# Hybrid decoder layer, first token tile: sums of squares by products with ones instead of a second load of the rows

## Chip, cores and metric

The kernel runs on one core of a Trainium2 chip. The metric is the device time of one execution in microseconds (us). Beside the plain runs there is one profiled execution with a trace of every engine and every transfer.

## What is computed

One layer on 2048 tokens of width 1024, all in float32. Every row of `x` is first divided by its root mean square; that scale is what the change is about:

```python
def rms_norm(x, w):
    xf = x.astype(jnp.float32)
    y = xf * lax.rsqrt(jnp.mean(xf * xf, axis=-1, keepdims=True) + EPS)
    return (y * w.astype(jnp.float32)).astype(x.dtype)

u = rms_norm(h, norm_pre_mix[i])
proj = u @ w_in[i]
q, k, v, qi, ki, wi, z, xbc, dt = jnp.split(proj, offsets, axis=-1)
```

The projection feeds a sparse attention (an indexer scores all keys, each query keeps its best 256) and a scanned state-space mixer with a short convolution. Their outputs go through one output projection, and a squared-ReLU MLP follows.

## The kernel before

The tokens are cut into four tiles of 512 (T), the 1024 channels into eight tiles of 128 (k). `in_proj(t)` makes, for one token tile, one small product called the misc product here (76 columns: index keys, index weights, step sizes) and 20 products of 128 columns with the tiles of `w_in`. In the back half each token tile gets `out_proj` and `mlp`. Attention, key selection and the scan are generators that `weave` steps beside that main sequence. The order of the instructions on each engine is not written by hand: a scheduler orders them by priorities and its own idea of their durations, and each engine then runs its list in that order, waiting where an operand is not there.

A float32 product is made of three products of rounded halves (`mm3`): high by high (L257), high by low in the moving operand (L260), low by high (L261). For each the moving operand is a channel tile of `x` with 512 tokens, the stationary one a tile of the weights. `moving(t)` (L295 to L313) makes the moving halves: it loads channel tile k of the transposed `x` (name `xr`, ring `wr` of four buffers that the weights share), ACT scales and rounds it to the high half, and DVE (k = 0, 1, 2, 4, 6) or, after one more pass on ACT, POOL (k = 3, 5, 7) makes the low half. `load_w` (L234) loads a half of a weight tile into the same ring and lets ACT (the misc weights) or POOL (L231, L232) make its halves in rings of two (`wh`, `wl`): the third half can only be made once the products that read the first are done.

The scale of the rows is not multiplied into `x`, but into the results. `row_scale(t)` (L276) loads the same 512 rows a second time, not transposed, as four tiles of 128 x 1024 (name `x_in`, ring `m4` of two), squares each on ACT with a sum along the row (L283), and `rsqrt` (L202) turns the four columns of sums into scales with ten small DVE instructions (L210 to L225). `row_spread` (L287) turns them with four products with the identity (`p_rs`, L290) into a tile with the scale along the columns, which DVE copies to `rsb` (L292). Every result is evicted with a multiplication by `rsb` (`scaled`, L329): first that of the misc product (`mi`), then that of each `w_in` product (`raw`). `mi` is transposed by PE (L343) and starts a long list on DVE (L345 to L360 and `softplus`, L437). The two PSUM banks named `mm` go round: misc product, `w_in` tile 0, tile 1, tile 2. Tile 1 needs the bank that `mi` has read; tile 2 needs the bank of tile 0, in which the convolution runs (L372, L374, last written to `pre`).

For token tile 0 all of this stands at the very start of the program; for the later tiles `row_scale(t + 1)` and `moving(t + 1)` are called in the tail of `in_proj(t)` (L429 to L434). `leave` (L525), a step of the scan, already sums squares by products with ones (L532): four products, each with a 128 x 128 tile of squares as the stationary operand and one column of ones as the moving one. All transfers are issued by SP (SyncE), in the order of its list; `late_constants` (L135) loads small constants, `dsk` in two transfers, `dtb` and `nega` among them, and ACT takes the exponential of `nega` (L153).

Of the kernel before, what the change touches and what calls it, by code (L numbers as in the profile page):

```python
# [8 lines left out]
F32 = mybir.dt.float32  # L9
# [6 lines left out]
AF = mybir.ActivationFunctionType  # L16
# [5 lines left out]
P = 128  # L22
L = 2048
D = 1024
T = 512
NT = L // T
NB = T // P
KT = D // P
# [13 lines left out]
def hybrid_layer(ctx, tc, x, x_t, w_cols, n_post_mix, n_post_mlp, w_in, w_misc, dt_bias, a_log, d_skip,  # L42
                 w_out, w_up, w_down, rel_bias, c_ident, c_flip, c_stack, c_tri, c_trineg, c_caus, c_bucket, out, dbg=None):
    nc = tc.nc
    V, S, G, PE, SP = nc.vector, nc.scalar, nc.gpsimd, nc.tensor, nc.sync

    cp = ctx.enter_context(tc.tile_pool(name="cp", bufs=1))
# [27 lines left out]
    def place(tag):  # L75

        if tag in rings:
            rings[tag].append(rings[tag].pop(0))
            return rings[tag][-1]
        return where[tag]  # L80

    def tl(tag, shape, dt=F32, name=None):
        pool, bufs, slot = place(tag)
        return pool.tile(shape, dt, tag=name if tag in ("s", "ks", "ssm") else slot, name=name or tag, bufs=bufs)
# [9 lines left out]
    def once_tile(name, shape, dt=F32):  # L94
        return where["ssm"][0].tile(shape, dt, name=name, bufs=1)
# [6 lines left out]
    def pt(tag, name=None):  # L102
        pool, bufs, slot = place(tag)
        return pool.tile([P, 512], F32, tag=slot, name=name or tag, bufs=bufs)
# [6 lines left out]
    def const(ap, shape, name, dt=F32):  # L111
        t = cp.tile(shape, dt, name=name)
        SP.dma_start(t, ap)
        return t
# [14 lines left out]
    junk_m = cp.tile([P, 512], I8, name="junk_m")  # L129
    tiny = cp.tile([P, 1], F32, name="tiny")  # L130
    V.memset(tiny, 1.17549435e-38)
    w_pm, w_pl, w_ssd = cols[:, 0:8], cols[:, 8:16], cols[:, 56:60]
    cn = {}

    def late_constants():  # L135

        cn["tri"] = once_tile("tri", [P, P])
        SP.dma_start(cn["tri"], c_tri)
        cn["trineg"] = once_tile("trineg", [P, P])
        SP.dma_start(cn["trineg"], c_trineg)  # L140
        cn["ones"] = once_tile("ones", [P, 1])
        V.memset(cn["ones"], 1.0)
        cn["stack"] = const(c_stack, [P, DH], "stack")
        cn["caus"] = const(c_caus, [P, P], "caus")
        dsk = cn["dsk"] = once_tile("dsk", [P, 4])
        for j in range(2):
            SP.dma_start(dsk[j * DH:(j + 1) * DH],
                         d_skip.rearrange("(m j) -> j m", j=2)[j:j + 1].partition_broadcast(DH))
        cn["dtb"] = once_tile("dtb", [P, H])
        SP.dma_start(cn["dtb"], dt_bias.rearrange("(o h) -> o h", o=1).partition_broadcast(P))  # L150
        nega = cn["nega"] = once_tile("nega", [P, H])
        SP.dma_start(nega, a_log.rearrange("(o h) -> o h", o=1).partition_broadcast(P))
        S.activation(nega, nega, AF.Exp)  # L153
        V.tensor_scalar(nega, nega, -1.0, None, op0=OP.mult)
# [47 lines left out]
    def rsqrt(o, v, n, scale, who="s", work=None, also=None):  # L202


        if work is None:
            xx, u = (tl(who, [P, n], name=name) for name in ("rs_x", "rs_u"))
        else:
            xx, u = work[:, 0:n], work[:, n:2 * n]
        yi = tl(who, [P, n], I32, name="rs_y")
        V.tensor_scalar(xx, v, scale, EPS, op0=OP.mult, op1=OP.add)  # L210
        if also is not None:
            V.scalar_tensor_tensor(xx, also, scale, xx, op0=OP.mult, op1=OP.add)
        V.tensor_scalar(yi, xx.bitcast(I32), -0.5, float(0x5f3759df), op0=OP.mult, op1=OP.add)
        y = yi.bitcast(F32)
        q = tl(who, [P, n], name="rs_q")

        V.tensor_tensor(u, xx, y, op=OP.mult)
        V.tensor_tensor(u, u, y, op=OP.mult)
        V.tensor_scalar(q, u, 0.375, -1.25, op0=OP.mult, op1=OP.add)
        V.tensor_tensor(u, u, q, op=OP.mult)  # L220
        V.scalar_tensor_tensor(y, u, 1.875, y, op0=OP.add, op1=OP.mult)

        V.tensor_tensor(u, xx, y, op=OP.mult)
        V.scalar_tensor_tensor(u, u, -0.5, y, op0=OP.mult, op1=OP.mult)
        V.scalar_tensor_tensor(o, u, 1.5, y, op0=OP.add, op1=OP.mult)  # L225
# [25 lines left out]
    state = {"win": "0"}  # L251
# [24 lines left out]
    def row_scale(t):  # L276

        ss = tl("s", [P, NB], name="ss")
        for b in range(NB):
            xt = tl("m4", [P, D], name="x_in")  # L280
            r0 = t * T + b * P
            SP.dma_start(xt, x[r0:r0 + P, :])
            S.activation(xt, xt, AF.Square, accum_out=ss[:, b:b + 1])  # L283
        rs = state["rs", t] = tl("s", [P, NB], name="rs")
        rsqrt(rs, ss, NB, 1.0 / D)

    def row_spread(rs, tag="mm"):  # L287
        p = pt(tag, "p_rs")
        for b in range(NB):
            PE.matmul(p[:, b * P:(b + 1) * P], rs[:, b:b + 1].broadcast_to([P, P]), ident, start=True, stop=True)  # L290
        rsb = tl("rsb", [P, T])
        V.tensor_copy(rsb, p)  # L292
        return rsb

    def moving(t):  # L295

        us = state["u", t] = []
        for k in range(KT):
            d = tl("u", [P, 2, T], F32R)
            raw = tl("wr", [P, T], name="xr")  # L300
            SP.dma_start(raw, x_t[t, :, k, :])
            wk = w_pm[:, k:k + 1]
            if str(k) in MG:
                if MG[0] == "a":
                    S.activation(raw, raw, AF.Copy, scale=wk)
                else:
                    G.tensor_scalar(raw, raw, wk, None, op0=OP.mult)
                S.activation(d[:, 0, :], raw, AF.Copy)
                G.tensor_tensor(d[:, 1, :], raw, d[:, 0, :].bitcast(F32), op=OP.subtract)  # L309
            else:  # L310
                S.activation(d[:, 0, :], raw, AF.Copy, scale=wk)  # L311
                V.scalar_tensor_tensor(d[:, 1, :], raw, wk, d[:, 0, :].bitcast(F32), op0=OP.mult, op1=OP.subtract)  # L312
            us.append(d)  # L313
# [6 lines left out]
    def in_proj(t):  # L320
        t0 = t * T
        w = None
        if t == 0:
            w = load_w(w_misc, [P, KT, 76], '11')
            moving(0)
        else:
            rsb = row_spread(state["rs", t], TB)
        u = state["u", t]
# [2 lines left out]

        p = proj(w_misc, u, w, how=HI_)
        if t == 0:
            row_scale(0)
            rsb = row_spread(state["rs", 0], "acc")
        mi = tl("m2", [76, T], name="mi")
        scaled(mi, p[0:76])
        if t == 0:
            late_constants()
        yield 5.2  # L340
        p = pt(TB, "p_tr")
# [12 lines left out]
        sq = tl("m2", [P, NB, DH], name="sq")  # L354
# [9 lines left out]
        for m in range(8):  # L364
            p = proj(w_in[m], u, how=HI_)
            raw = tl("m2", [P, T + 4], name="raw")
# [8 lines left out]
            if m == 1:  # L375
                p = pt(TB, "p_tr")
# [21 lines left out]
        for m in range(4):  # L398
            p = proj(w_in[8 + m], u, how=HI_)
# [9 lines left out]
        p = proj(w_in[12], u, how=HI_)  # L409
# [8 lines left out]
        p = proj(w_in[13], u, how=HI_)  # L418
# [3 lines left out]
        p = pt(TB, "p_tr")  # L422
# [8 lines left out]
        for m in range(2, 6):  # L431
            queries(m)
            if m == 5 and t + 1 < NT:
                moving(t + 1)  # L434
            yield 5.2
# [22 lines left out]
    def ssd(t):  # L458
# [4 lines left out]
        p = pt(bank, "p_cs")  # L463
# [5 lines left out]
        p = pt(bank, "p_cs")  # L469
# [55 lines left out]
        def leave(c, sis):  # L525

            p = pt(bank, "p_ms")
            for g, si in enumerate(sis):
                ys, sq = si[:, 0:2], si[:, 2:4]
                S.activation(sq, ys, AF.Square)  # L530
                for j in range(2):
                    PE.matmul(p[:, g:g + 1], sq[:, j], cn["ones"], start=j == 0, stop=j == 1)  # L532
            rs = tl("ssm", [P, 2], name="rs_s")
            rsqrt(rs, p[:, 0:2], 2, 1.0 / 256, "ssm", p[:, 2:6])
            for g, si in enumerate(sis):
                ys, yp = si[:, 0:2], si[:, 2:6].rearrange("p (s j) t -> p s j t", s=2).bitcast(F32R)
                sl = slice((g + 1) * P, (g + 2) * P)
                PE.matmul(p[:, sl], rs[:, g:g + 1].broadcast_to([P, P]), ident, start=True, stop=True)
                for j in range(2):
                    V.scalar_tensor_tensor(ys[:, j], ys[:, j], w_ssd[:, 2 * g + j:2 * g + j + 1], p[:, sl],  # L540
                                           op0=OP.mult, op1=OP.mult)
                S.activation(yp[:, 0], ys, AF.Copy)
                V.tensor_tensor(yp[:, 1], ys, yp[:, 0].bitcast(F32), op=OP.subtract)
                r0, t0 = 512 + 256 * g, t * T + c * P
                for s in range(2):
                    SP.dma_start(mix_d[s, r0:r0 + 256, t0:t0 + P].rearrange("(j p) t -> p j t", p=P), yp[:, s].bitcast(F32))
# [541 lines left out]
```

## Time and profile before

| | us |
|---|---|
| median of three runs | 2925.88 |
| lowest and highest of them | 2923.69, 2927.11 |
| the profiled execution, its own time | 2928.29 |
| its span, first to last instruction | 2926.5 |

In the profile, PE is the matrix engine, PEld its weight loads, DVE the vector engine, ACT the scalar engine, POOL GpSimd, SP the engine that issues the transfers. All times are counted from the start of the span. In the timeline a row gives start, duration, engine, line, operation, output and inputs, how many instructions were merged, and in square brackets how long the engine sat idle before and what ended that. One float32 product with a whole float32 operand (lines 290, 343, 532) shows as two records. Products overlap: their rate is read from the distance of their starts, not from their durations.

### The profile page before, as it was taken

What the parts mean: (1) busy time and instruction counts of PE and PEld (TensorE: products, weight loads), DVE (VectorE), ACT (ScalarE), POOL (GpSimd) and SP (SyncE); (2) the same over time, 40 slices, a digit from 0 to 9 for tenths busy, and PEclk for the clock granted to TensorE, in tenths of its full rate; (3) what the DMA queues carried; (4) which work ended last, traced back from release to release, by engine and by line L of the source; (5) the groups of instructions that cost most, each with busy time, mean ns of one, the idle gap of its engine ahead of it and who ended that gap; (6) DMA issues with size and microseconds to landing.
All of it is one profiled execution on the core that took longest, in us unless ns stands there. A gap on an engine that the chain in (4) does not pass through costs nothing.

```text
span 2926.5 us, 41201 instructions
## 1 busy us (share of the span) xinstructions
PE 2761.9 (94%) x13558; PEld 2250.7 (77%) x13558; DVE 1642.4 (56%) x4106; ACT 1481.5 (51%) x2550; POOL 1762.6 (60%) x1721
## 2 busy tenths in 40 slices
PE   7988989789989999998999999999999999999998
PEld 5766767667768887887787888878888888778886
DVE  5479588888575666747765565666444342511113
ACT  2375477675837575677773847644332332311101
POOL 4666556667666656654456575644564656588775
PEclk8999989999989999999999999999999999999999
DMA  3765654634733333255223222553222225522222
GB/s 128 224 189 151 218 157 149 208 118 160 249 120 119 112 103 102 90 176 180 101 94 98 90 97 79 170 177 102 87 95 81 93 78 177 204 95 97 95 94 86
DMA packets 286741, 383.46 MB, mean 131 GB/s; under 512 B 26520, under 2 KB 151360, under 8 KB 286528
## 3 DMA queue, kind: packets, MB, share of 16 engines
q1 hardware_dynamic: 286528, 380.84, 40.0%
q8 instruction: 107, 1.75, 0.2%
q14 instruction: 106, 0.87, 0.1%
HBM read 316.44 MB, written 64.30 MB: 130 GB/s over the span
## 4 chain that ended last, share of the span: by engine, by line
PE 67%; DVE 13%; ACT 6%; DMA 5%; issue 4%; POOL 3%; SPq 1%; POOLq 0%; DVEq 0%; ACTq 0%
PE p_mm L257 9%; PE p_mm L261 9%; PE p_mm L260 9%; PE p_dn L260 7%; PE p_dn L261 7%; PE p_dn L257 7%; ACT junk_k L610 5%; PE p_o L725 4%; PE p_s L683 4%; PE p_pt L717 3%; POOL wl L232 2%; PE p_ix L591 1%; DVE cnd L618 1%; PE p_acc L260 1%; PE p_acc L257 1%
## 5 line engine op out<-in xcount | busy, mean ns | idle before, releaser
L232 POOL TENSOR_TENSOR wl<-wr,wh 128x512 fp32r<-128x512 f32 (+1 forms) x740 | 987.0, 1335 | 179.6 <-ACT wh L229 107.0
L231 POOL TENSOR_SCALAR wh<-wr 128x512 fp32r<-128x512 f32 x674 | 449.6, 667 | 752.1 <-PE p_mm L260 372.8
L257 PE MATMUL p_mm<-u,wh 128*128 128x512 f32 (+1 forms) x1696 | 685.4, 404 | 47.4 <-ACT u L311 15.4
L261 PE MATMUL p_mm<-u,wl 128*128 128x512 f32 (+1 forms) x1696 | 682.8, 404 | 13.2 <-POOL wl L232 12.9
L260 PE MATMUL p_mm<-u,wh 128*128 128x512 f32 (+1 forms) x1696 | 674.9, 398 | 0.6 <-POOL u L309 0.3
L610 ACT ACTIVATE junk_k<-sc,cnd 128x512 int8<-128x512 f32 (+10 forms) x434 | 576.4, 1328 | 157.8 <-DVE cnd L618 122.2
L257 PEld LDWEIGHTS p_mm<-u,wh 128*128 128x128 f32 (+1 forms) x1696 | 322.9, 190 | 119.3 <-ACT u L311 17.5
L260 PE MATMUL p_dn<-wl,g 128*128 128x512 f32 x1008 | 402.2, 399 | 4.2 <-POOL wl L232 4.2
L261 PE MATMUL p_dn<-wh,g 128*128 128x512 f32 x1008 | 399.5, 397 | 2.7 <-POOL g L836 2.7
L261 PEld LDWEIGHTS p_mm<-u,wl 128*128 128x128 f32 (+1 forms) x1696 | 322.5, 190 | 88.7 <-POOL wl L232 21.3
L260 PEld LDWEIGHTS p_mm<-u,wh 128*128 128x128 f32 (+1 forms) x1696 | 322.6, 190 | 69.6 <-DVE u L312 2.3
L257 PE MATMUL p_dn<-wh,g 128*128 128x512 f32 x1008 | 328.0, 398 | 1.9 <-POOL wh L231 1.3
L834 ACT ACTIVATE r<-r 128x512 f32<-128x512 f32 x128 | 80.4, 629 | 437.1 <-DVE r L833 436.7
L688 DVE CUSTOM_DVE_ANT_0 pp<-p_s,mk 128x512 f32<-128x512 f32 (+3 forms) x320 | 192.5, 607 | 134.3 <-PE p_s L683 130.5
L719 ACT ACTIVATE ppt<-p_pt 128x512 fp32r<-128x512 f32 (+1 forms) x288 | 155.3, 568 | 208.1 <-PE p_pt L717 170.0
L720 DVE TENSOR_TENSOR ppt<-p_pt,ppt 128x512 fp32r<-128x512 f32 (+1 forms) x288 | 182.6, 655 | 129.6 <-ACT ppt L719 126.9
L260 PEld LDWEIGHTS p_dn<-wl,g 128*128 128x128 f32 x1008 | 190.3, 189 | 46.8 <-POOL wl L232 5.5
L261 PEld LDWEIGHTS p_dn<-wh,g 128*128 128x128 f32 x1008 | 190.3, 189 | 43.8 <-POOL g L836 3.1
L257 PEld LDWEIGHTS p_dn<-wh,g 128*128 128x128 f32 x1008 | 185.8, 189 | 42.0 <-POOL wh L231 2.9
L725 PE MATMUL p_o<-ppt,VV 128*128 128x256 f32 x1088 | 211.1, 294 | 1.9 <-DVE ppt L720 1.0
L617 DVE TENSOR_SCALAR keep<-cnt 128x1 int32<-128x1 f32 (+1 forms) x341 | 70.2, 206 | 244.1 <-ACT junk_k L610 242.7
L836 POOL TENSOR_TENSOR g<-r,g 128x512 fp32r<-128x512 f32 x128 | 170.1, 1331 | 53.2 <-ACT g L835 51.9
(253 smaller groups left out, 4177.6 us busy)
## 6 DMA issues: line engine op xcount, KB each, us to landing
wr<-w_up SPq DMA_DIRECT2D x256, 256.0 KB, 2.6
wr<-w_down SPq DMA_DIRECT2D x256, 256.0 KB, 2.6
wr<-w_in SPq DMA_DIRECT2D x160, 256.0 KB, 2.9
tq<-toep_d SPq DMA_DIRECT2D x128, 128.0 KB, 2.6
qs<-q_d SPq DMA_DIRECT2D x256, 64.0 KB, 2.5
wr<-w_out SPq DMA_DIRECT2D x64, 256.0 KB, 3.7
mix<-mix_d SPq DMA_DIRECT2D x32, 512.0 KB, 8.1
q_d<-qp SPq DMA_DIRECT2D x24, 512.0 KB, 3.6
```

The source lines that it names most:

```text
L231: G.tensor_scalar(dst_hi, src_f, 1.0, 0.0, op0=OP.mult, op1=OP.add)
L232: G.tensor_tensor(dst_lo, src_f, dst_hi.bitcast(F32), op=OP.subtract)
L257: m = PE.matmul(o, ah, bh, start=first, stop=False)
L260: PE.matmul(o, ah, bl, start=False, stop=False)
L261: state["mm3"] = PE.matmul(o, al, bh, start=False, stop=last).ins.name
L610: S.activation(junk_k[:, 0:n], scs[j], AF.Sign, bias=bias(j), accum_out=cnt[:, j:j + 1])
L683: PE.matmul(p[:, 0:w], qs[:, var, hh, :], K1[:, g, j0:j0 + w], start=var == 0, stop=var == 1)
L688: V.tensor_tensor_reduce(out=pp[:, j0:j0 + w], in0=p[:, 0:w], in1=mk[:, j0:j0 + w], scale=1.0, scalar=-3e38, op0=OP.add, op1=OP.max, accum ...
L719: S.activation(pg[:, 0, 0:w], p[:, 0:w], AF.Copy)
L720: V.tensor_tensor(pg[:, 1, 0:w], p[:, 0:w], pg[:, 0, 0:w].bitcast(F32), op=OP.subtract)
L725: PE.matmul(po[:, c0:c0 + 256], VV[:, kk, g, :], pg[:, part, j * 256:(j + 1) * 256], start=kk == 0 and part == 0, stop=kk == nb - 1 and pa ...
L836: G.tensor_tensor(gt[:, 1, :], r, gt[:, 0, :].bitcast(F32), op=OP.subtract)
```

## The change

For token tile 0, `moving(0, sums)` squares each channel tile right after its load (ACT, a new 128 x 512 tile `sq0` of the ring `m4`), and PE multiplies it with a column of ones: for each k four products, one for each block of 128 tokens, with the squares as the stationary operand. The eight k are summed in PSUM (`p_ss`, a bank of the pair `acc`). `rsqrt` reads those four columns and keeps its two work tiles in the same bank. `row_scale(0)` and its four loads of `x_in` are gone. The column of ones is made once at the start, in another pool, and `leave` uses it too. Token tiles 1 to 3 are as before.

```diff
+    ones = cp.tile([P, 1], F32, name="ones")
+    V.memset(ones, 1.0)
...
-        cn["ones"] = once_tile("ones", [P, 1])
-        V.memset(cn["ones"], 1.0)
...
-    def moving(t):
+    def moving(t, sums=None):
...
             SP.dma_start(raw, x_t[t, :, k, :])
+            if sums is not None:
+                sq = tl("m4", [P, T], name="sq0")
+                S.activation(sq, raw, AF.Square)
+                for b in range(NB):
+                    PE.matmul(sums[:, b:b + 1], sq[:, b * P:(b + 1) * P], ones, start=k + b == 0, stop=k == KT - 1 and b == NB - 1)
...
             w = load_w(w_misc, [P, KT, 76], '11')
-            moving(0)
+            sums = pt("acc", "p_ss")
+            moving(0, sums)
...
         if t == 0:
-            row_scale(0)
+            rs = state["rs", 0] = tl("s", [P, NB], name="rs")
+            rsqrt(rs, sums[:, 0:NB], NB, 1.0 / D, work=sums[:, 4:4 + 2 * NB])
             rsb = row_spread(state["rs", 0], "acc")
...
-                    PE.matmul(p[:, g:g + 1], sq[:, j], cn["ones"], start=j == 0, stop=j == 1)
+                    PE.matmul(p[:, g:g + 1], sq[:, j], ones, start=j == 0, stop=j == 1)
```

The scheduler orders the whole program anew. Three places of its lists follow, as they stand before and now.

On PE, the end of the misc product and the beginning of the second half of `w_in` tile 0. Before (`p_mm_152` is the misc product, `p_mm_309` tile 0):

```order
L261 MATMUL p_mm_309<-u_124,wl_299 128x512
L260 MATMUL p_mm_152<-u_146,wh_104 76x512
L261 MATMUL p_mm_152<-u_146,wl_105 76x512
L257 MATMUL p_mm_309<-u_130,wh_304 128x512
L260 MATMUL p_mm_309<-u_130,wh_304 128x512
L343 MATMUL p_tr_233<-ident_77,mi_212 128x76 x4
```

Now (`p_mm_203` is the misc product, `p_mm_343` tile 0, `p_ss` the sums):

```order
L261 MATMUL p_mm_343<-u_145,wl_333 128x512
L306 MATMUL p_ss_111<-ones_83,sq0_183 128x1 x4
L306 MATMUL p_ss_111<-ones_83,sq0_194 128x1 x4
L260 MATMUL p_mm_203<-u_168,wh_106 76x512
L261 MATMUL p_mm_203<-u_168,wl_107 76x512
L257 MATMUL p_mm_203<-u_180,wh_106 76x512
L260 MATMUL p_mm_203<-u_180,wh_106 76x512
L261 MATMUL p_mm_203<-u_180,wl_107 76x512
L257 MATMUL p_mm_203<-u_191,wh_106 76x512
L260 MATMUL p_mm_203<-u_191,wh_106 76x512
L261 MATMUL p_mm_203<-u_191,wl_107 76x512
L257 MATMUL p_mm_343<-u_157,wh_338 128x512
```

The last two groups of products with ones (k = 6 and 7), and eight products of the misc product where two were left, now stand behind the first half of tile 0 and ahead of its second half.

On PE, the products that spread the row scale (`p_rs`, L290). Before, behind the first two products of tile 0:

```order
L257 MATMUL p_mm_309<-u_109,wh_298 128x512
L260 MATMUL p_mm_309<-u_109,wh_298 128x512
L257 MATMUL p_mm_152<-u_146,wh_104 76x512
L290 MATMUL p_rs_205<-ident_77,rs_190 128x128 x4
L261 MATMUL p_mm_309<-u_109,wl_299 128x512
L257 MATMUL p_mm_309<-u_114,wh_298 128x512
```

Now, behind all 24 products of tile 0 (`p_mm_388` is tile 1, L351 the transposes of `mi`, L343 before):

```order
L260 MATMUL p_mm_343<-u_191,wh_338 128x512
L261 MATMUL p_mm_343<-u_191,wl_339 128x512
L290 MATMUL p_rs_241<-ident_77,rs_228 128x128 x4
L351 MATMUL p_tr_267<-ident_77,mi_248 128x76 x4
L257 MATMUL p_mm_388<-u_112,wh_377 128x512
L260 MATMUL p_mm_388<-u_112,wh_377 128x512
```

The spreading has moved from the beginning of tile 0 to its end, and tile 1 follows the transposes of `mi`.

On SP, the transfers ahead of the first weights of `w_in` (`xr` are the channel tiles, in order of k). Before, from k = 4 on:

```order
L301 DMA xr<-x_t 128x512 x2
L113 DMA stack<-c_stack 128x64
L282 DMA x_in<-x 128x1024
L113 DMA caus<-c_caus 128x128
L147 DMA dsk<-d_skip 64x4x1
L282 DMA x_in<-x 128x1024
L147 DMA dsk<-d_skip 64x4x1
L150 DMA dtb<-dt_bias 128x8
L301 DMA xr<-x_t 128x512
L152 DMA nega<-a_log 128x8
L301 DMA xr<-x_t 128x512
L246 DMA wr<-w_in 128x512 x24
```

Now, from k = 2 on:

```order
L113 DMA stack<-c_stack 128x64
L301 DMA xr<-x_t 128x512 x2
L113 DMA caus<-c_caus 128x128
L147 DMA dsk<-d_skip 64x4x1
L301 DMA xr<-x_t 128x512
L147 DMA dsk<-d_skip 64x4x1
L301 DMA xr<-x_t 128x512 x2
L150 DMA dtb<-dt_bias 128x8
L152 DMA nega<-a_log 128x8
L301 DMA xr<-x_t 128x512
L246 DMA wr<-w_in 128x512 x24
```

The loads of `x_in` are gone. The small transfers `dsk`, `dtb` and `nega` now stand between the loads of the last four channel tiles, where before they stood between those of `x_in`. On ACT the exponential of `nega` stands ahead of the squares of k = 4 to 7.

## Rows read from the trace of the kernel before

**Rows 1.** The page, part 1: busy time, share of the span, instructions of each engine.
```profile
PE 2761.9 (94%) x13558; PEld 2250.7 (77%) x13558; DVE 1642.4 (56%) x4106; ACT 1481.5 (51%) x2550; POOL 1762.6 (60%) x1721
```

**Rows 2.** Busy time by stretch: stretch, length, engines (instructions), PE clock granted, DMA share, GB/s.
```profile
0.00:48.00 48.00, 27.86 (x85) 16.85 (x86) 21.50 (x59) 14.99 (x25) 17.19 (x22) 0.86 0.47 151
...
100.00:900.00 800.00, 714.56 (x3617) 564.42 (x3616) 595.51 (x1606) 512.35 (x1066) 500.09 (x505) 0.95 0.55 177
900.00:2926.50 2026.50, 1967.61 (x9636) 1627.25 (x9635) 991.31 (x2381) 944.85 (x1447) 1209.07 (x1157) 0.99 0.34 113
```

**Rows 3.** Chain of waits, first 60 us: start, duration, what.
```profile
4.01 7.06 DMA x_in<-x
...
17.11 6.91 DMA xr<-x_t
...
27.61 1.17 DVE rs_u L224
28.78 6.13 issue
34.93 0.64 POOL wh L231
```

**Rows 4.** Timeline of DVE and PE: scale tile, first eviction, first product of tile 2.
```profile
31.16 0.69 DVE L292 COPY rsb<-p_rs 128x512 f32<-128x512 f32 x1 [2.17 <-PE p_rs L290]
35.51 0.69 DVE L329 TENSOR_TENSOR mi<-p_mm,rsb 76x512 f32<-76x512 f32 x1 [3.65 <-PE p_mm L261]
...
47.72 0.47 PE L257 MATMUL p_mm<-u,wh 128*128 128x512 f32 x1 [2.74 <-DVE rs_y L221]
```

**Rows 5.** Busy time of one stretch (as in 2), then PE's timeline at either rate.
```profile
24.00:30.00 6.00, 4.07 (x10) 2.34 (x11) 4.02 (x8) 2.17 (x4) 3.12 (x3) 0.50 0.36 118
...
33.06 0.63 PE L260 MATMUL p_mm<-u,wh 128*128 128x512 f32 x1
33.48 0.63 PE L261 MATMUL p_mm<-u,wl 128*128 128x512 f32 x1
...
38.00 0.39 PE L260 MATMUL p_mm<-u,wh 128*128 128x512 f32 x1
38.23 0.40 PE L261 MATMUL p_mm<-u,wl 128*128 128x512 f32 x1
```

**Rows 6.** PE's timeline: products with ones at either rate, and products that spread a scale.
```profile
189.93 0.95 PE L532 MATMUL p_ms<-ones,si 128*128 128x1 f32 x8
...
632.67 1.87 PE L532 MATMUL p_ms<-ones,si 128*128 128x1 f32 x8 [2.07 <-DVE st L519]
...
29.05 2.08 PE L290 MATMUL p_rs<-ident,rs 128*128 128x128 f32 x8 [1.03 <-DVE rs L225]
```

**Rows 7.** ACT: timeline of the first channel tile, and the page's group of squares.
```profile
6.26 0.72 ACT L311 ACTIVATE u<-xr,cols 128x512 fp32r<-128x512 f32 x1 [0.90 <-DMA xr<-x_t]
...
L834 ACT ACTIVATE r<-r 128x512 f32<-128x512 f32 x128 | 80.4, 629 | 437.1 <-DVE r L833 436.7
```

**Rows 8.** POOL's timeline: weight halves of tile 0 and 1.
```profile
34.93 1.21 POOL L231 TENSOR_SCALAR wh<-wr 128x512 fp32r<-128x512 f32 x2 [6.15 <-issue]
36.10 2.52 POOL L232 TENSOR_TENSOR wl<-wr,wh 128x512 fp32r<-128x512 f32 x2
```

**Rows 9.** Transfers issued in the first 60 us (KB each, us to landing), rate of 8 to 12 us.
```profile
wr<-w_in SPq DMA_DIRECT2D x12, 256.0 KB, 2.6
...
x_in<-x SPq DMA_DIRECT2D x4, 512.0 KB, 7.1
...
dsk<-d_skip SPq DMA_DIRECT2D x2, 1.0 KB, 8.6
...
DMA packets 863, 1.49 MB, mean 373 GB/s; under 512 B 102, under 2 KB 342, under 8 KB 863
```

**Rows 10.** Who waited for whom on PE, 100 to 900 us: total, times, longest.
```profile
PE p_y L514 <- DVE lm L503: 10.9, 6, 4.8
PE p_x L496 <- DMA si<-s_d: 8.6, 6, 5.3
```

## The prediction

> **What bounds the kernel now.** I read the page first: PE is busy 94% of the span [rows 1], so a stretch is worth what it keeps PE from working. The busy time by stretch says where PE does not work [rows 2]: from 900 us on it is idle 2026.5 - 1967.6 = 59 us of 2026, from 100 to 900 us 85 of 800, and in the first 48 us, in which all of this change lies, 48 - 27.9 = 20. The chain of waits of that start [rows 3] shows why: 7.1 us for a load of `x_in`, 6.9 us for the second last channel tile, then the row scale on DVE. The entry called issue (6.1 us) is POOL waiting until PE has finished the misc product, whose weight buffers it needs.
>
> The timeline gives the two points that count. `mi`, the first eviction, starts at 35.51; `rsb` had been copied at 31.16, and the last product was what it waited for [rows 4]. From `mi` on DVE is the bound: its list of small instructions ends in the convolution of tile 0, and only then has tile 2 a bank, at 47.72. So `mi` to tile 2 takes 47.72 - 35.51 = 12.2 us, and PE stands still for the last 2.74 of them. What the change is worth is read from when `mi` can start.
>
> The third thing is PE's rate. After the wait for the late channel tiles its granted clock is 0.50 in 24 to 30 us, that is 1.2 GHz, and wide products (512 moving columns) follow each other at 33.48 - 33.06 = 0.42 us; at 2.4 GHz at 38.23 - 38.00 = 0.23 [rows 5]. I count 0.43 and 0.23.
>
> **What goes.** Four loads of 512 KB and, on ACT, four squares of 128 x 1024. ACT gets eight squares of 128 x 512 at about 0.63 us each [rows 7], 5.0 us, about what the four took, so I set ACT's work at nothing. The loads are 2.1 MB; while many transfers were under way the chip moved 373 GB/s [rows 9], so they held the others up by at most 2.1 MB / 373 GB/s = 5.6 us. That would be the gain if nothing took their place.
>
> **What comes.** Eight groups of four products with ones. `leave` does the same four in 0.95 us at the fast clock and in 1.87 us at the slow one [rows 6]: 7.6 or 15.0 us in all. Some of this falls into PE's idle time, which is why the order on PE has to be followed.
>
> PE can begin when the first squares are there: the first tile was in ACT at 6.26 [rows 7], and its square now goes first, so at 6.26 + 0.63 = 6.9. Up to the group of k = 5 the list holds six such groups and 15 wide products. At the slow clock that is 6 x 1.87 + 15 x 0.43 = 17.7 us, to 24.6. Is the data there in time? The squares of k = 4 stand behind the exponential of `nega` on ACT. The issue of `nega` comes at about 11 us (behind the wait for k = 2 and two small issues). It lands between 2.6 and 8.6 us later: the nearest rows are a weight tile on a quiet queue, and `dsk`, 1 KB, that waited among the loads of `x_in` [rows 9]. I take the middle of the upper half, 7 us, 18. PE wants the group of k = 4 at 6.9 + 4 x 1.87 + 15 x 0.43 = 20.8. So the loads have slack, and PE itself is the bound. The Trainium skill, page "DMA: Bandwidth & Descriptors", section "Rules for kernel authors", says that a transfer whose last dimension is strided becomes one descriptor per element. The slow landing of so small a `dsk` agrees with that; by the page alone that wait is its own, stays when `x_in` goes, and now stands ahead of four channel tiles, which speaks against the change and against the first rival below.
>
> Then come 13 wide products, 12 of tile 0 and one of the misc product. Here PE has been working without a gap, and I take eight of them slow and five fast: the rows at 33.06 and 38.00 show that the clock came back after a run of wide products [rows 5]. 8 x 0.43 + 5 x 0.23 = 4.6, to 29.2. Two groups with ones at the fast clock, 1.9, to 31.1; eight products of the misc product, 1.85, to 32.9. Before, this was at 35.5. So far it is 2.6 us better.
>
> Now the order takes this back. POOL makes the second half of tile 0's weights, 0.6 and 1.3 us (half of the pairs in [rows 8]), and the third product can start at 32.9 + 1.9 = 34.8; ten more at 0.23 end at 37.1. Only then do the products that spread the scale come: 1.0 us at the fast clock (2.08 at the slow one, [rows 6]), to 38.1. `rsb` takes 0.69 [rows 4], and `mi` starts at 38.8. The small instructions of `rsqrt` are no bound: the sums are ready at 31.1, and ten of them, of which one or two could take 1.17 us [rows 3], are done by 35.
>
> So `mi` starts 38.8 - 35.5 = 3.3 us later, though PE has then done 12 more products of tile 0. That credit is lost again, because tile 2 waits for DVE: tile 1 is done about 7 us after `mi`, and DVE needs its 12.2. DVE's list there has one eviction of 0.69 us more and four small instructions fewer; I leave it at 12.2, with 0.7 to either side for the range. Tile 2 starts at 38.8 + 12.2 = 51.0, **3.3 us later** than before, and from there on the main sequence runs as it did. The column of ones made earlier, the other bank of the pair `acc` and the work tiles in PSUM I cost at nothing: they lie in engines that wait there.
>
> The profiled execution took 2928.29 us, 2.4 more than the median of 2925.88; with 3.3 it would take 2931.6, and the median **2929.2 us**. About 0.2%, 5.9 us, is what a measurement of this kernel can tell from no change: faster is below 2920.0, slower above 2931.7.
>
> **Rivals.** *The loads bound the start.* PE gets its fast clock within the first groups, the products with ones vanish in its waits, and what is left is the load of the last channel tile, earlier by up to 5.6 us. For it: the chain of waits is made of loads until 24 us [rows 3]. Against it: PE gets four products more for each channel tile, and the scale now comes last. 2925.9 - 5.6 = 2920.3, with DVE's 0.7 just below 2920; a half of this case counts as faster.
>
> *PE stays at 1.2 GHz until `mi`.* The groups with ones stand between the wide products now, and the fast clock may not come in that stretch. It decides at the 13 wide products: if these do not see the fast clock, 24.6 + 5.6 + 3.7 + 3.4 = 37.3, POOL 1.9, ten products 4.3, the spreading 2.1, `rsb` 0.7: `mi` at 46.3, 10.8 later, 2936.7. For it: the group of `leave` that ran after a wait took 1.87 [rows 6]. Against it: the clock did come back in a similar run before.
>
> *The new order elsewhere.* Both lists run alike up to about the 160th transfer, then attention, key selection and scan are woven in at other places up to the third token tile of the back half. PE's 85 idle us between 100 and 900 [rows 2] are made of waits such as those for the scan's loads and masks, single ones up to 5.3 us [rows 10]. Three or four of these more or fewer are 10 us: 2939 or, with luck, 2919. Nothing in the lists says which; side work stands a little earlier now.
>
> **Numbers.** Forecast 0.47; loads 0.16; slow clock 0.13; order against 0.13; order in favour 0.11, which I count as faster. Faster is 0.11 and half of 0.16, 0.19, rounded to 0.20. Slower is 0.13 + 0.13 and the upper end of the forecast, 0.30. The rest, 0.50, is no difference. The range reaches from a little below the loads' case, 2919, to the unlucky order, 2939.
>
> **What would show it.** Right: groups of products with ones at 1.87 us up to about 25 us; the misc product done near 33; the products of the row scale near 37; `mi` near 39, tile 2 near 51 us; POOL waiting for PE near 31, no wait for a channel tile over 2 us on PE after 10 us. Wrong: `mi` before 35, or PE waiting for `nega` or the last channel tile, or a shift from the first 51 us that differs from the one at the end of the span: then the order elsewhere has decided.

## The result and the profile after

The changed kernel takes 2953.19 us (median of 5 runs, 2944.22 to 2959.87), the kernel before 2926.73 us (5 runs, 2923.69 to 2931.19): ratio 1.0086, 95% interval 1.0062 to 1.0110. It is **slower by 26 us**, where I had forecast 2929.2 and a range that ended at 2939. The profiled execution of the change took 2947.63 us, its span is 2945.7. Three executions of all that follow (one of the kernel before, one each of two versions) took 6329 to 10494 us and are left out of every median and ratio.

The page of the changed kernel, part 1, against [rows 1]; then the busy time of the three stretches of [rows 2] (columns as there):

```profile
PE 2776.7 (94%) x13622; PEld 2264.0 (77%) x13622; DVE 1651.6 (56%) x4106; ACT 1483.8 (50%) x2550; POOL 1766.5 (60%) x1721
```
```profile
0.00:48.00 48.00, 36.40 (x154) 30.01 (x155) 18.41 (x59) 16.20 (x26) 17.58 (x22) 1.00 0.37 112
100.00:900.00 800.00, 708.83 (x3559) 560.33 (x3559) 596.43 (x1579) 505.96 (x1053) 489.01 (x496) 0.94 0.56 174
900.00:2945.70 2045.70, 1981.73 (x9694) 1633.55 (x9692) 1002.21 (x2407) 953.12 (x1460) 1223.35 (x1167) 0.99 0.35 113
```

In the first 48 us PE is busy 8.5 us more than before, for 69 records more. From 100 to 900 us it gets through 58 records fewer than before in the same time, and what is left over then makes the last stretch 19.2 us longer. So the loss does not lie where the diff does.

**The head**, PE's and DVE's timeline of the changed kernel (L306: products with ones; four are recorded as eight):

```profile
6.67 1.86 PE L306 MATMUL p_ss<-ones,sq 128*128 128x1 f32 x8 [6.67 <-ACT sq L304]
...
19.71 3.41 PE L306 MATMUL p_ss<-ones,sq 128*128 128x1 f32 x16
22.98 0.77 PE L257 MATMUL p_mm<-u,wh 128*128 128x512 f32 x1
...
27.39 0.63 PE L257 MATMUL p_mm<-u,wh 128*128 128x512 f32 x1
27.82 0.45 PE L260 MATMUL p_mm<-u,wh 128*128 128x512 f32 x1
...
28.33 1.84 PE L306 MATMUL p_ss<-ones,sq 128*128 128x1 f32 x16
...
31.90 0.39 PE L257 MATMUL p_mm<-u,wh 128*128 128x512 f32 x1
...
34.62 1.05 PE L290 MATMUL p_rs<-ident,rs 128*128 128x128 f32 x8
...
46.57 0.47 PE L257 MATMUL p_mm<-u,wh 128*128 128x512 f32 x1 [3.34 <-DVE tails L377]
```
```profile
32.02 0.16 DVE L225 SCALAR_TENSOR_TENSOR rs<-p_ss,rs_y 128x4 f32<-128x4 f32 x1
35.71 0.69 DVE L292 COPY rsb<-p_rs 128x512 f32<-128x512 f32 x1 [3.53 <-PE p_rs L290]
36.44 0.69 DVE L336 TENSOR_TENSOR mi<-p_mm,rsb 76x512 f32<-76x512 f32 x1
```

PE works from 6.67 us without a gap until the products of the row scale end, near 35.7. `mi` starts at 36.44, 0.9 later than before [rows 4], and tile 2 at 46.57, 1.15 **earlier** than before, not 3.3 later.

**Where the time goes.** For what follows I count the 8928 main products (L257, L260, L261) in the order in which they ran, and compare stretches that hold the same ones. Products 576 to 672 are four weight tiles of the second token tile. Before, and in the changed kernel:

```profile
208.20:243.50 35.30, 34.39 (x200) 28.05 (x199) 34.30 (x110) 26.69 (x72) 21.81 (x26) 1.00 0.55 165
```
```profile
204.60:255.10 50.50, 42.90 (x238) 34.24 (x238) 47.04 (x156) 36.85 (x99) 24.09 (x27) 0.90 0.50 144
```

The same 96 products take 15.2 us more. The changed order has put 38 more records of side work on PE and 46 more on DVE into this stretch, and DVE was full there already: 34.3 of 35.3 us before, 47.0 of 50.5 after. (As full a DVE did not hold PE up before; that its added work makes the waits is read from this one place, and no run tests it alone.) PE's timeline of the changed kernel shows the place:

```profile
220.08 0.40 PE L261 MATMUL p_mm<-u,wl 128*128 128x512 f32 x1
220.31 0.41 PE L691 MATMUL p_s<-K,qs 128*128 128x256 f32 x2
...
222.85 0.38 PE L733 MATMUL p_o<-ppt,VV 128*128 128x256 f32 x1
225.05 0.62 PE L733 MATMUL p_o<-ppt,VV 128*128 128x256 f32 x3 [1.81 <-DVE ppt L728]
...
228.72 0.87 PE L504 MATMUL p_x<-ident,si 128*128 128x128 f32 x3 [2.70 <-issue]
...
230.25 1.70 PE L540 MATMUL p_ms<-ones,si 128*128 128x1 f32 x8
232.25 0.90 PE L725 MATMUL p_pt<-ident,pp 128*128 128x128 f32 x3 [0.30 <-ACT pp L706]
232.81 0.77 PE L257 MATMUL p_mm<-u,wh 128*128 128x512 f32 x1
233.38 0.63 PE L260 MATMUL p_mm<-u,wh 128*128 128x512 f32 x1
233.81 0.63 PE L261 MATMUL p_mm<-u,wl 128*128 128x512 f32 x1
```

From 220.08 to 232.81 PE gets no main product: in its list stand products of the scan (`p_y`, `p_x`, `p_ms`) and of attention (`p_s`, `p_o`, `p_pt`), and while one of them waits, for DVE or (2.70 us) for something that the trace does not name, no main product behind it runs. Then the main products follow each other at 0.43 us, the slow rate, and the granted clock of this stretch is 0.50:

```profile
225.90:236.10 10.20, 7.19 (x28) 6.34 (x27) 10.14 (x30) 6.62 (x18) 2.62 (x3) 0.50 0.37 112
```

In the kernel before, the same scan steps have main products between them, and the longest time without one in this stretch is 2.7 us:

```profile
224.19 0.70 PE L517 MATMUL p_st<-xd 128*128 128x256 f32 x2
224.54 0.58 PE L257 MATMUL p_mm<-u,wh 128*128 128x512 f32 x1
224.96 0.28 PE L725 MATMUL p_o<-ppt,VV 128*128 128x256 f32 x1
225.07 0.40 PE L260 MATMUL p_mm<-u,wh 128*128 128x512 f32 x1
```

This is one place of several. From product 576 to product 2304, before (661.9 us) and after (678.2 us), each in two rows:

```profile
208.20:453.50 245.30, 219.09 (x1161) 175.19 (x1160) 195.13 (x545) 144.18 (x331) 137.36 (x146) 0.95 0.57 173
453.50:870.10 416.60, 369.61 (x1862) 290.80 (x1860) 316.99 (x810) 282.61 (x544) 276.01 (x271) 0.94 0.52 171
```
```profile
204.50:468.60 264.10, 235.46 (x1225) 188.61 (x1226) 210.81 (x600) 164.16 (x374) 139.75 (x148) 0.92 0.55 163
468.60:882.70 414.10, 363.12 (x1813) 285.21 (x1812) 310.70 (x775) 265.77 (x506) 272.92 (x271) 0.94 0.53 170
```

PE's records are about as many (3023 and 3038), but 16.3 us are lost: 6.4 as idle time (73.2 before, 79.6 after) and 9.9 as longer busy time (588.7 and 598.6), with the granted clock at 0.92 in place of 0.95 in the first row. The Trainium skill, page "TensorE: Matmul & The Clock Gate", section "HAM oscillation — how this bites in real kernels", describes waits for transfers after which the products restart at half rate, so that a wait costs more than itself. This trace agrees in the restart, with 0.43 us between products after the waits above, though the wait that it names there (1.81 us) is one for DVE.

### The profile page after: what moved, and what is told of

It reads as the page before. It is cut to its first block, busy times and chain, and to the rows that moved or that the text cites. A ratio compares the mean times of both kernels' runs of the same rounds, so it can differ in the third digit from the quotient of the medians.

```text
span 2945.7 us, 41345 instructions
## 1 busy us (share of the span) xinstructions
PE 2776.7 (94%) x13622; PEld 2264.0 (77%) x13622; DVE 1651.6 (56%) x4106; ACT 1483.8 (50%) x2550; POOL 1766.5 (60%) x1721
## 4 chain that ended last, share of the span: by engine, by line
PE 67%; DVE 12%; ACT 6%; DMA 5%; POOL 5%; issue 4%; SPq 1%; POOLq 0%; DVEq 0%; ACTq 0%
PE p_mm L257 10%; PE p_mm L261 10%; PE p_mm L260 10%; PE p_dn L260 7%; PE p_dn L261 7%; PE p_dn L257 7%; ACT junk_k L618 4%; PE p_o L733 4%; PE p_s L691 3%; PE p_pt L725 3%; POOL wl L232 3%; PE p_ix L599 2%; POOL wh L231 2%; DVE cnd L626 1%; PE p_acc L257 1%
## 5 line engine op out<-in xcount | busy, mean ns | idle before, releaser
L257 PE MATMUL p_mm<-u,wh 128*128 128x512 f32 (+1 forms) x1696 | 685.2, 404 | 32.7 <-POOL wh L231 17.3
L261 PE MATMUL p_mm<-u,wl 128*128 128x512 f32 (+1 forms) x1696 | 682.0, 403 | 12.4 <-POOL wl L232 12.3
L260 PE MATMUL p_mm<-u,wh 128*128 128x512 f32 (+1 forms) x1696 | 674.8, 398 | 0.0
L260 PE MATMUL p_dn<-wl,g 128*128 128x512 f32 x1008 | 403.0, 400 | 5.5 <-POOL wl L232 5.5
L257 PEld LDWEIGHTS p_mm<-u,wh 128*128 128x128 f32 (+1 forms) x1696 | 324.5, 191 | 104.6 <-POOL wh L231 24.4
L261 PE MATMUL p_dn<-wh,g 128*128 128x512 f32 x1008 | 399.4, 396 | 2.8 <-POOL g L844 2.8
L261 PEld LDWEIGHTS p_mm<-u,wl 128*128 128x128 f32 (+1 forms) x1696 | 323.3, 191 | 90.3 <-POOL wl L232 21.3
L260 PEld LDWEIGHTS p_mm<-u,wh 128*128 128x128 f32 (+1 forms) x1696 | 323.8, 191 | 66.7 <-issue 0.4
L257 PE MATMUL p_dn<-wh,g 128*128 128x512 f32 x1008 | 329.3, 399 | 6.3 <-POOL wh L231 5.4
L260 PEld LDWEIGHTS p_dn<-wl,g 128*128 128x128 f32 x1008 | 190.4, 189 | 49.5 <-POOL wl L232 8.5
L261 PEld LDWEIGHTS p_dn<-wh,g 128*128 128x128 f32 x1008 | 190.4, 189 | 43.3 <-POOL g L844 3.2
L257 PEld LDWEIGHTS p_dn<-wh,g 128*128 128x128 f32 x1008 | 184.8, 188 | 48.3 <-POOL wh L231 8.7
L706 ACT ACTIVATE pp<-pp,nm 128x128 f32<-128x128 f32 (+15 forms) x128 | 153.4, 1198 | 107.7 <-DVE nm L703 95.4
```

Source lines behind the costliest of these rows:

```text
L257: m = PE.matmul(o, ah, bh, start=first, stop=False)
L260: PE.matmul(o, ah, bl, start=False, stop=False)
L261: state["mm3"] = PE.matmul(o, al, bh, start=False, stop=last).ins.name
L706: S.activation(pp, pp, AF.Exp, bias=nm, accum_out=den[:, h:h + 1])
```

## The experiments

Two theories. **Order**: the edited head is worth about nothing, and the loss comes from the places that the scheduler gives all later work, because its simulated times move. **Head**: the edit itself costs, by its products, its PSUM banks or a state that it leaves behind. Within the first, a narrower one: attention's products, which stand on average some 60 main products (14 us) earlier in PE's list than before, make the loss.

**Holding the order.** Edges of issue order alone (no semaphore) make each engine issue everything behind the head in the order of a table. The core of the edit, cut (`mine` are the instructions of one engine, `at` the next place in its table):

```
+        for s in steps.split(","):
...
+            now = mine[-1 - at]
+            if last is not None:
+                tc.add_manual_dep(now, last.name, nosync, reason="order")
+            last = now
```

The table is the order that the scheduler gave to one of the two kernels, so head and order can be exchanged. In the traces of both exchanges the lists behind the head are those of the table on all five engines, but for six records on PE in the first.

*New head, old order.*

> The changed kernel, with every engine held behind the head to the issue order of the kernel before. If the order elsewhere made the loss: the head's own worth alone, 0 to 1.2 us below the kernel before (the trace of the change has the products of tile 2 1.15 us earlier), so 2925 to 2927, ratio 0.999 to 1.001. If the head itself or what it leaves behind (the other bank of the pair, the slower start of a later stage) made it: 2945 to 2960, as the change.

Measured: 2927.06 us against 2927.05, ratio 1.0005 (0.9995 to 1.0015).

*Old head, new order.*

> The kernel before, with every engine held behind the head to the issue order of the changed kernel. If the order made the loss: 2945 to 2960, ratio 1.006 to 1.011, and a spread between runs as wide as the change's (15 us). If the head made it: 2924 to 2931.

Measured: 2953.66 us, ratio 1.0089 (1.0075 to 1.0104). The two settle the main question: with the old order the changed head costs nothing that can be measured (the interval leaves room for -1.5 to 4.4 us), and with the new order the head with the old code loses all of it. Which engine's order makes the loss stays open: the table holds all five at once. Products 576 to 672, new head with old order and old head with new order:

```profile
207.00:242.30 35.30, 34.39 (x200) 28.05 (x199) 34.12 (x110) 26.69 (x72) 21.75 (x25) 1.00 0.56 167
```
```profile
211.20:262.40 51.20, 43.48 (x237) 34.68 (x238) 46.89 (x155) 36.87 (x99) 24.98 (x27) 0.90 0.49 140
```

The stretch goes with the order, to a tenth of a us with the old one, whichever head ran ahead of it.

*Where in the program.* The table is made of one order up to a main product and of the other behind it, all with the new head. Old order up to product 720, then new:

> The changed kernel, in the old order up to main product 720 (about 275 us), in the new order after it. The trace puts 13 of 18.5 us between products 576 and 720. If these 13 us are a loss that stays: 13 us less than the change, 2938 to 2943. If the later places lose as much whatever came before: 2945 to 2955. If the whole loss hangs on that first place: 2925 to 2930.

Measured: 2942.35 us, ratio 1.0053 (1.0040 to 1.0067). New order up to product 720, then old:

> The counterpart: the changed kernel in the new order up to main product 720, then in the old one. If the 13 us between products 576 and 720 stay: 2937 to 2942. If slack later takes them back: 2925 to 2931.

Measured: 2931.90 us, ratio 1.0016 (1.0005 to 1.0027). The first place alone costs 5 us, not 13: behind it the old order makes up for part. Products 576 to 1008, before, and in this run the stretches 576 to 672 and 576 to 1008:

```profile
208.20:387.30 179.10, 156.29 (x819) 124.56 (x818) 135.16 (x366) 97.36 (x226) 102.13 (x106) 0.96 0.62 191
```
```profile
201.00:252.90 51.90, 43.66 (x238) 34.48 (x238) 49.34 (x154) 36.77 (x99) 24.36 (x27) 0.89 0.48 141
...
201.00:386.70 185.70, 162.64 (x835) 129.88 (x835) 140.98 (x382) 98.86 (x230) 104.34 (x107) 0.92 0.60 184
```

Of 51.9 - 35.3 = 16.6 us lost up to product 672, 185.7 - 179.1 = 6.6 are left at product 1008: what was done early need not be done later. With the new order behind it (the run before) the same start is worth 11 us, so the parts do not simply add here.

Old order up to product 2304, then new:

> The changed kernel in the old order up to main product 2304 (all of the projection, 870 us), in the new order for the back half. By the trace of the change 12.5 of its 18.5 us are there by product 2304, so 6 to 13 us of loss are left: 2932 to 2940. If the loss hangs on one place in the first 870 us: 2924 to 2930.

Measured: 2935.66 us, ratio 1.0034 (1.0024 to 1.0044). (Product 2304 lies in the first MLP tiles; the projection itself ends with product 2016.) New order up to product 2304, then old:

> The counterpart: new order up to main product 2304, old order for the back half. 12 to 18 us of loss by the trace: 2937 to 2945, and with the run before 26 us together. If the back half's slack takes it back, as the old order took back the first 13 us: 2925 to 2931.

Measured: 2942.10 us, ratio 1.0056 (1.0042 to 1.0070). So 16 us belong to the first 870 us and 10 to the back half, together the 26. No single place holds the loss.

**Is it attention's place?** Four kernels whose order is the scheduler's own. First, the loads kept:

```
             SP.dma_start(raw, x_t[t, :, k, :])
             if sums is not None:
+                if k % 2:
+                    xt = tl("m4", [P, D], name="x_in")
+                    SP.dma_start(xt, x[k // 2 * P:(k // 2 + 1) * P, :])
                 sq = tl("m4", [P, T], name="sq0")
```

> The changed kernel with the four loads of the rows put back among the channel tiles, unused. The head then carries the work of both kernels. By its lists this one has attention's products on PE where the kernel before has them (on average 2 main products off; the changed kernel has them 56 earlier). If the place of attention in PE's list makes the loss: 2925 to 2933, though it loads and multiplies more. If the loss comes from the products with ones, or the order has no such meaning: 2945 to 2960.

Measured: 2951.54 us, ratio 1.0087 (1.0069 to 1.0105). Attention stood where it did before, and the loss is there all the same, so **the narrower theory falls**. Products 576 to 672 in this kernel:

```profile
209.70:261.10 51.40, 44.06 (x242) 35.61 (x242) 47.94 (x154) 36.98 (x99) 23.89 (x27) 0.90 0.50 144
```

It has the change's stretch without a main product, record for record, from 225.29 to 238.02:

```profile
225.29 0.40 PE L261 MATMUL p_mm<-u,wl 128*128 128x512 f32 x1
...
230.26 0.63 PE L736 MATMUL p_o<-ppt,VV 128*128 128x256 f32 x3 [1.81 <-DVE ppt L731]
...
233.94 0.87 PE L507 MATMUL p_x<-ident,si 128*128 128x128 f32 x3 [2.71 <-issue]
...
238.02 0.78 PE L257 MATMUL p_mm<-u,wh 128*128 128x512 f32 x1
```

Then the window of the scan, one setting of the plan, in the changed kernel (`SS` is when the scan of the first token tile starts and ends, in us of the plan's own time):

```
-    SS = (90,170)
+    SS = (92,172)
```

> The changed kernel with one number of the plan changed: the window of the scan 92 to 172 in place of 90 to 170. Attention's products on PE stand 1 main product from their old places, the scan's 22 off. If attention's place decides: 2925 to 2935. If the scan's waits for its loads decide, which my prediction had in mind: anything from 2920 to 2960, and not as the kernel before. If the head decides: 2945 to 2960.

Measured: 2930.37 us, ratio 1.0011 (1.0000 to 1.0021). A window moved by 2 us in the plan takes back most of the loss without a table. The same line as `SS = (95,175)` in the kernel before:

> The kernel before, its head untouched, with the window of the scan 95 to 175: attention's products stand 50 main products earlier than in the kernel before, close to the changed kernel's places (13 off). If attention's early place makes the loss: 2940 to 2965. If it needs the new head: 2922 to 2932.

Measured: 2943.52 us, ratio 1.0056 (1.0038 to 1.0073): the kernel before loses two thirds as much by that setting of its plan, with no edit in the head. Last, the products with ones added to the kernel before (besides this only a second tile `ones` is made at the start, and `moving` takes `sums`):

```
+            if sums is not None:
+                sq = tl("m4", [P, T], name="sq0")
+                S.activation(sq, raw, AF.Square)
+                for b in range(NB):
+                    PE.matmul(sums[:, b:b + 1], sq[:, b * P:(b + 1) * P], ones, start=k + b == 0, stop=k == KT - 1 and b == NB - 1)
...
-            moving(0)
+            moving(0, pt("acc", "p_ss"))
```

> The kernel before with the eight squares and the 32 products with ones added and their sums unused; loads and row scale as they were. Attention's products stand 25 main products earlier than before, between the two. If the place decides, about half of the loss: 2932 to 2945. If the head carries through, its price alone, 3 to 15 us by the rows of the products: 2930 to 2942, with the shift there already at 60 us and the same at the end.

Measured: 2952.16 us, ratio 1.0091 (1.0073 to 1.0109). That is more than attention's place or the head's price foretold, and the place above has little part in it: products 576 to 672 take 39.7 us in its trace. Its head price is in the trace too, at product 144 (the start of tile 5): before, changed kernel, old head with new order, loads kept, products with ones added to the old head, a row of PE's timeline each:

```profile
66.20 0.39 PE L257 MATMUL p_mm<-u,wh 128*128 128x512 f32 x1
```
```profile
65.87 0.39 PE L257 MATMUL p_mm<-u,wh 128*128 128x512 f32 x1
```
```profile
72.21 0.39 PE L257 MATMUL p_mm<-u,wh 128*128 128x512 f32 x1
```
```profile
69.81 0.39 PE L257 MATMUL p_mm<-u,wh 128*128 128x512 f32 x1
```
```profile
73.59 0.39 PE L259 MATMUL p_mm<-u,wh 128*128 128x512 f32 x1
```

By these rows the four loads cost 3.9 us (69.81 - 65.87) and the added products 7.4 (73.59 - 66.20), where the row scale still waits for the loads. Both sizes are rough: in the other traces of the new head this point lies at 62.54 to 65.92, and PE's fast rate begins at another time in each (last section).

**Another order that is better?** The changed kernel with `SS = (88,168)` and with `SS = (93,173)`.

> The changed kernel with the window of the scan 88 to 168: another order, attention 3 main products off its old places, key selection 9, the scan 20. If each order has waits of its own that no distance from the old one foretells: between 2918 and 2955, and it may be the first below the kernel before. If nearness of attention and key selection is what counts: 2925 to 2932.

Measured: 2936.48 us, ratio 1.0036 (1.0022 to 1.0049).

> The same with 93 to 173: attention 4, key selection 14, the scan 30 main products off. As before: 2918 to 2955 if the order is a draw, 2926 to 2934 if nearness counts.

Measured: 2938.45 us (four executions), ratio 1.0047 (1.0033 to 1.0061). Nearness to the old order does not foretell the time: in the traces attention and key selection stand nearer to their old places with 88 than with 92 (the scan farther), yet 92 is the faster. Of all the orders tried, which gave 2930 to 2954 us, none is below the old one, and no version beats the kernel before. That the plan's settings were fitted to the old head's times would explain it; no run tests that.

## Why the prediction was wrong, step by step

**The step that failed** is the end of its working: "Tile 2 starts at 51.0, 3.3 us later than before, and from there on the main sequence runs as it did." The main sequence did not: behind the head another order runs, and from 200 us on it costs 26 us. The text had this as its third rival, with a chance of 0.13 and 10 us. Its price was mis-sized. I took three or four waits of up to 5 us from [rows 10] in the first 900 us. The exchange of the order shows 16 us there, and 10 more in the back half, where I had looked for nothing. I also counted idle time alone, though between products 576 and 2304 9.9 of the 16.3 us are busy time. And I looked for the waits on PE's own side (loads, masks), while the place that the rows show is one where DVE was full and got more to do. Why the new order is the worse one at the other places stays open. The sign that I had named, a shift of the first 51 us that differs from the one at the end, is what came: 1.15 us earlier at tile 2, 19 later at the end of the span.

**The head, term by term.**
- PE begins at 6.67 (I had 6.9), runs at the slow rate and is its own bound, as forecast. That holds for this trace: in another execution of this head the fast rate came early, and there PE waited 1.86 us for POOL's first weight half of tile 0 (at 20.48). Groups with ones cost less where they follow other work: 16 records in 3.27 us, start to start, at the slow rate, so 1.64 for four products (I took 1.87 from [rows 6]), and 1.70 for two groups at the fast one, 0.85 for four (0.95). The group of k = 5 is done at 22.98, not 24.6.
- The fast rate came at 27.8: eleven of the 13 wide products were slow, where I had taken eight. The rival in which PE stays slow until `mi` fell here. When the fast rate comes is luck that no count of products foretold (last section). The misc product is done at 31.90, not 32.9.
- POOL's 1.9 us did not exist. I had read the 6.1 us called issue in [rows 3] as a wait for the misc product. In the changed kernel POOL's second half of tile 0 starts right behind the last product of tile 0's first half (28.11), and the wait for the misc product comes with tile 1. Before, it was the same: POOL started at 34.93 [rows 8], behind the last product of that first half (34.62), while the misc product's last one started at 35.07. So PE goes on at 31.90 with twelve products without a gap:

```profile
28.42 0.62 POOL L231 TENSOR_SCALAR wh<-wr 128x512 fp32r<-128x512 f32 x1 [1.80 <-issue]
...
31.93 0.63 POOL L231 TENSOR_SCALAR wh<-wr 128x512 fp32r<-128x512 f32 x1 [1.53 <-PE p_mm L260]
```

- The spreading products come last on PE, behind tile 0, as forecast: `rs` is ready at 32.2 and they start at 34.62. `mi` follows at 36.44 (forecast 38.8).
- DVE took 46.57 - 36.44 = 10.1 us from `mi` to tile 2, not the 12.2 that I carried over. Before, three small instructions of that list (L348, L447, L213) took 1.27, 0.96 and 1.26 us that took 0.17, 0.18 and 0.17 in the changed kernel; there one (L377, 0.15 before) took 1.27. Why some are slow is not shown.
- The exponential of `nega` waited for its load until 16.44 (I had 18) and held no product up: PE has no gap from 6.67 to 35.7. `dsk`, from which I had taken that price, landed in 5.3 us in the changed kernel, 8.6 before [rows 9]; the difference went with the loads of `x_in`. What is left is twice the 2.6 us of a weight tile. I had put such a wait down to the stride of `dsk`, but `dtb`, 4 KB and not strided, took 5.4 beside it (9.2 before): these rows do not show that the stride makes it slow.
- The loads that went were worth 3.9 us by the rows above, roughly (bounded at 5.6, then set at nothing). The rival "the loads bound the start" had this gain; it did not see that the products with ones take it back, nor the order.

**Carrying a head's shift to the end** was wrong in itself. With the new order, the old head stood 6.3 us behind the new one at product 144 (72.21 and 65.87), and the medians differ by 0.5 us (2953.66 and 2953.19). At product 1728 the two stood at 678.0 and 676.7 us: within the first quarter, 5 of the 6.3 us were gone.

## What to carry to other kernels

Where a scheduler places instructions by simulated times, an edit at the start is two changes: itself, and a new order of everything behind it. Compare the lists of both kernels before costing the edit, and where they part, hold the old order by edges on the changed kernel: that measures the edit alone, and the difference measures the order. A control that takes back one part of the edit (here the loads) gets an order of its own too, so its time alone says nothing about the part.

## What was not expected of the hardware

- The same list ran at another rate in another execution. The run with the new order up to product 720 has, up to there, the changed kernel's list on every engine. The changed kernel first, then that run, same products:

```profile
15.10 0.63 PE L261 MATMUL p_mm<-u,wl 128*76 128x512 f32 x1
15.53 1.70 PE L306 MATMUL p_ss<-ones,sq 128*128 128x1 f32 x8
```
```profile
14.06 0.40 PE L261 MATMUL p_mm<-u,wl 128*76 128x512 f32 x1
14.29 0.95 PE L306 MATMUL p_ss<-ones,sq 128*128 128x1 f32 x8
```

  The next product follows after 0.43 us in the one and 0.23 in the other. PE had worked without a gap since 6.67 and 6.37, yet the fast rate came at 27.8 in the changed kernel and by 13.8 in that run. Tile 2 starts at 46.57 and 43.27.
- The column of the granted clock does not show this slow start. The changed kernel from 6 to 28 us:

```profile
6.00:28.00 22.00, 21.33 (x75) 17.79 (x76) 4.57 (x7) 12.23 (x20) 6.51 (x6) 1.00 0.43 132
```

  It says 1.00, while wide products follow each other at 0.43 us until 27.82, the rate of 1.2 GHz. The events themselves are not wrong here: the first one in this trace is a rise at 27.93, and in that of the kernel before a rise at 17.36, where its products turn fast (17.34). The column takes off only slow stretches that an event opened, and so holds 1.00 ahead of the first event. The Trainium skill, page "TensorE: Matmul & The Clock Gate", section "Seeing it yourself", says not to trust the recorded clock events without a check; the spacing of the products is such a check, and here it agrees with the events and not with the column.
- The five runs of the changed kernel spread over 15.7 us, and in the order of their times the mean granted clock falls: 0.976 (2944.22 us), 0.975, 0.973, 0.972, 0.971 (2959.87 us). Other versions do not show this: new head with old order ran 2930.04 us at 0.970 and 2935.12 at 0.973. The old head under the new order spread over only 9 us in 4 runs, so the wide spread that I had expected of that order was not seen there.
